# Paged latent cache and its join in a two-layer decoder step: the turned halves first, all score products in a row, the samples' output projection in four column groups

## The chip, the cores and the metric

The kernel runs on one core of one Trainium2 chip. The metric is device time in microseconds from start to end of one execution; before the change the median of three executions is 3317.36 us (3316.31 to 3318.78).

## What is computed

One inference step of a small decoder: a gated DeltaNet layer with a ConvFFN, one shared latent key/value (MLA), then an MLA attention layer with a second ConvFFN. A prompt of 1024 tokens and 16 meta tokens, and eight samples of one token each, pass through together. All inputs are float32. The part of the change is the samples' attention over their paged past, 4096 positions each in 32 pages of 128, and the output projection after it:

```python
def latent_scores(q_lat, q_pe, c, k_rope):
    s = jnp.einsum('bqhr,bkr->bhqk', q_lat, c) + jnp.einsum('bqhd,bkd->bhqk', q_pe, k_rope)
    return s.astype(jnp.float32) * MLA_SCALE

def sample_attend(q_lat, q_pe, c, k_rope, c_past, k_past):
    ...
    s_past = latent_scores(q_lat, q_pe, c_past, k_past)
    ...
    prob = jax.nn.softmax(jnp.concatenate([s_past, s_new], axis=-1), axis=-1).astype(c.dtype)
    return (jnp.einsum('bhqk,bkr->bqhr', prob[..., :P], c_past)
            + jnp.einsum('bhqk,bkr->bqhr', prob[..., P:], c))

    o = jnp.einsum('blhr,rhv->blhv', o_lat, w_uv).reshape(B, L, MLA_HEADS * MLA_V)
    return o @ w_out
```

Here r is the latent rank 256, the rope part has 64 entries, there are 8 heads, and w_out is 1024 x 1024.

## The kernel before

The program is written with a scheduler that fixes each engine's order before the run; every engine then works through its own queue strictly in that order, waiting on semaphores. `merge` gives the order in which pieces of several streams are written down: each stream yields a number, and the stream with the lowest number goes on. Near the end of the attention layer two streams are merged: `cache_all` (the samples' cache) and `outp` (the main output projection of the prompt, tile name `psop`, 576 products in three groups of heads and three chunks of tokens, accumulated into `acc`).

`cache_all` runs 16 units: eight samples b, two halves gp of 2048 positions each. `cache_unit` (L1463) does this:

- POOL gathers two blocks `cg` of 1 MB of latent rows (L1468) and one block `krt` of 0.5 MB of rope rows (L1471), through the page table. `cg` has four buffers, so two units are on the chip; `krt` has two.
- TensorE transposes `krt` in two blocks of four into PSUM (`dkt`, L1476), and VectorE copies them to `krT`.
- For each half k of the latent rank, TensorE makes 16 transposes of `cg` in four blocks (`dct_`, L1487), which ScalarE (L1491) and VectorE (L1489) copy in turn to a tile `cT` of two buffers. Then it makes four products of 32 x 512 into the score tile `dscr` (L1493), one per group j of 512 positions: the stationary side is the query, 32 columns wide, and each product uses its own 32 columns of the array (`tile_position=(0, 32 * j)`). All of `dkt`, `dct_`, `dpt` and the join's small products share three PSUM buffers (`dtr`).
- After the second half four rope products with 64 rows follow (L1497).
- Softmax over the half: row maximum (VectorE L1502), exponential with sum (ScalarE L1506), four transposes of p (`dpt`, L1510), one copy, and sixteen products p by latent (`pv`, 32 x 256, L1516), again in four column groups. `OS`, `MX` and `LS` keep the running output, maximum and sum per sample.

After the last unit `join` (L1540) runs as one piece: maxima and sums are turned (`dj`), scores of the new token are added (`dsn`), a chain of small VectorE and ScalarE steps gives the weights, which are turned (`dfw`, L1574); the groups are combined (`dol`, L1584 and L1586), the value projection follows (`dov`, L1591), and then the output projection: for each head a block `wos` of w_out (0.5 MB, two buffers, those of `krt`) is loaded by SP (L1597), and two products of 8 x 512 per head gather the eight samples' rows (`dop`, L1599). The result is copied (`ys`, L1602), turned in eight transposes (`dopt`, L1605) and stored in the first eight columns of `acc[0]`.

Behind it come the rest of `outp`, the post-norm of the three chunks (`boundaries`) and the second ConvFFN. `fpst` (L945) are transposes of state rows that this ConvFFN needs.

Of the kernel before, what the change touches and what calls it, by code (L numbers as in the profile page):

```python
# [11 lines left out]
F32 = mybir.dt.float32  # L12
# [8 lines left out]
P = 128  # L21
# [40 lines left out]
def tile_step(ctx: ExitStack, tc: tile.TileContext, I, O, stop=None):  # L62
# [1382 lines left out]
    with ExitStack() as e2:  # L1445
# [17 lines left out]
        def cache_unit(b, gp):  # L1463
# [14 lines left out]
            sc = scp.tile([P, 512], F32, tag="sc", name="dscr")  # L1478
            for k in range(2):
                yield  # L1480
                cT = sp.tile([P, 4, 512], F32, tag="cT", name="cT")
                for gg in range(2):
                    for hf in range(2):
                        pt = dtr("dct_")
                        for i in range(4):
                            o = (2 * i + hf) * KVL + P * k
                            PE.transpose(pt[:, P * i:P * i + P], cg[gg][:, o:o + P], ident)  # L1487
                        if hf:
                            V.tensor_copy(cT[:, 2 * gg + hf, :], pt)  # L1489
                        else:  # L1490
                            A.copy(cT[:, 2 * gg + hf, :], pt)  # L1491
                for j in range(4):
                    PE.matmul(sc[32 * j:32 * j + 32, :], ql[:, k, b, :], cT[:, j, :], start=(k == 0), stop=False,  # L1493
                              tile_position=(0, 32 * j))
            for j in range(4):
                hf = j % 2
                PE.matmul(sc[32 * j:32 * j + 32, :], qr_s[64 * hf:64 * hf + 64, b, :],  # L1497
                          krT[64 * hf:64 * hf + 64, j // 2, :], start=False, stop=True, tile_position=(64 * hf, 32 * j))
# [34 lines left out]
        def cache_all(p0, p1):  # L1533
            for u in range(2 * NS):
                for f, _ in enumerate(cache_unit(u // 2, u % 2)):
                    yield p0 + (p1 - p0) * (u + f / 4.0) / (2 * NS)
            yield p1
            join()

        def join():  # L1540
# [31 lines left out]
            V.tensor_tensor(sn, sn, mm, op=ALU.mult)  # L1572
            ps = dtr("dfw")
# [6 lines left out]
            V.tensor_tensor(pn, sn[:, 0:H].unsqueeze(1).to_broadcast([NS, NS, H]), bc(ident[:NS, :NS], [NS, NS, H]), op=ALU.mult)  # L1580
            olT = dc.tile([P, 2, NS, H], F32, name="olT")
            for k in range(2):
# [4 lines left out]
                V.tensor_copy(olT[:, k], ps)  # L1587
            ps = dtr("dov")[:, :H * NS].rearrange("p (h s) -> p h s", s=NS)
# [3 lines left out]
            V.tensor_copy(os_, ps)  # L1592

            ps = [dtr(f"dop{i}") for i in range(2)]
            for h in range(H):
                st = krp.tile([P, D], F32, tag="krt", name="wos")
                SP.dma_start(st, I["b_w_out"][0, P * h:P * h + P, :])  # L1597
                for i in range(2):
                    PE.matmul(ps[i][:NS, :], os_[:, h, :], st[:, 512 * i:512 * i + 512], start=(h == 0), stop=(h == H - 1))  # L1599
            yt = dc.tile([NS, D], F32, name="ys")  # L1600
            for i in range(2):
                V.tensor_copy(yt[:, 512 * i:512 * i + 512], ps[i][:NS])  # L1602
            ps = dtr("dopt")[:, :KT * NS].rearrange("p (m s) -> p m s", s=NS)
            for m in range(KT):
                PE.transpose(ps[:, m, :], yt[:, P * m:P * m + P], ident[:NS, :NS])  # L1605
            V.tensor_copy(acc[0][:, :, 0:NS], ps)
# [3 lines left out]
        os_ = dc.tile([P, H, NS], F32, name="os")  # L1610
# [5 lines left out]
        merge(cache_all(0, CA), outp(I["b_w_out"][0], og_d, groups, ogp, 0.05, 1.0, True, NS, 6))  # L1616
# [71 lines left out]
```

## Time and profile before

| | |
|---|---|
| median of three executions | 3317.36 us |
| the profiled execution | 3314.68 us, span 3312.9 us |
| TensorE busy | 3123.5 us, 94% of the span, 20846 products |
| VectorE / ScalarE / POOL busy | 2030.3 / 1254.9 / 862.2 us |
| chain that ended last | PE 76%, DVE 14%, DMA 3% |
| mean granted clock of TensorE | 0.975 of full speed |
| cache units | from 2150 us; last p-by-latent product until 2391.64 us |
| join's output projection until its result is stored | until 2440.7 us |

How to read it: the times in the rows are microseconds from the span's start, or ns where so marked. An engine is busy while one of its instructions is under way; a product that waits in the array still counts. PEld is the loading of weights into the array, which overlaps with products. A float32 product shows as two records. PEclk is the share of TensorE's full clock that was granted: 1.00 is 2.4 GHz, 0.50 is 1.2 GHz, values between them are a mix over time. SPq rows are issues of DMAs by SyncE.

### The profile page before, as it was taken

To read this page: it belongs to the slowest core of one execution; us is meant where nothing else is said; L and a number is where in the kernel's file an instruction comes from. 1 tells how busy PE (TensorE), PEld (TensorE's weight loads), DVE (VectorE), ACT (ScalarE), POOL (GpSimd) and SP (SyncE) were. 2 spreads that over 40 slices of the span, in tenths; PEclk is the share of its full clock that TensorE was granted. 3 is DMA by queue.
4 is the path that set the end of the run, shared out by engine and by line. 5 is a ranking of instruction groups with operands and counts; after the bars stand their busy time and mean duration, and the time that the engine had idled before them with its cause. 6 is when DMAs were issued, how large, how long until landed. Compare 5 with 4: busy or idle time off the path is not lost.

```text
span 3312.9 us, 52527 instructions
## 1 busy us (share of the span) xinstructions
PE 3123.5 (94%) x20846; PEld 2884.2 (87%) x20846; DVE 2030.3 (61%) x4139; ACT 1254.9 (38%) x2541; POOL 862.2 (26%) x1013
## 2 busy tenths in 40 slices
PE   7999999999899999999978999999998999999997
PEld 6888888888799999999967888856678999999996
DVE  4777777766864555555576676544557355555556
ACT  4656555563433222222334444433224322222223
POOL 1433222210342222322342111111105332322322
PEclk9999999999899999999989999999998999999999
DMA  3222222235321111111121000354432111111111
GB/s 107 62 65 69 64 67 59 72 105 176 96 66 46 39 52 49 48 46 39 45 86 44 25 27 28 108 189 184 159 102 84 46 46 45 46 45 52 46 39 66
DMA packets 267650, 235.08 MB, mean 71 GB/s; under 512 B 57919, under 2 KB 246597, under 8 KB 263285
## 3 DMA queue, kind: packets, MB, share of 16 engines
q1 hardware_dynamic: 260224, 189.69, 19.7%
q0 software_dynamic: 6912, 41.95, 3.4%
q8 instruction: 164, 2.69, 0.3%
q14 instruction: 82, 0.66, 0.1%
q10 hardware_dynamic: 268, 0.09, 0.0%
HBM read 198.84 MB, written 33.40 MB: 70 GB/s over the span
## 4 chain that ended last, share of the span: by engine, by line
PE 76%; DVE 14%; DMA 3%; issue 3%; ACT 2%; POOL 1%; SPq 0%; ACTq 0%; POOLq 0%; DVEq 0%
PE fps L228 9%; PE fps L229 9%; PE fps L227 9%; PE fdn L228 5%; PE fdn L227 5%; PE fdn L229 5%; PE psu L227 2%; PE psu L229 2%; PE po L1408 2%; PE psu L228 2%; PE dscr L1493 2%; DVE acc L287 2%; PE psop L227 1%; DVE tm L658 1%; DVE xs L660 1%
## 5 line engine op out<-in xcount | busy, mean ns | idle before, releaser
L144 POOL TENSOR_TENSOR ws<-ws,vec 128x1024 f32<-128x1024 f32 (+1 forms) x127 | 249.5, 1965 | 424.3 <-DMA ws<-in_f_w_up_dram 210.1
L228 PE MATMUL fps<-xfl,wh 128*128 128x384 f32 (+1 forms) x1056 | 343.7, 326 | 8.2 <-POOL xfl L295 8.1
L227 PE MATMUL fps<-xfh,wh 128*128 128x384 f32 (+1 forms) x1056 | 341.8, 324 | 8.0 <-ACT xfh L293 7.0
L228 PE MATMUL fps<-xbl,wh 128*128 128x384 f32 (+1 forms) x1056 | 343.6, 325 | 4.8 <-POOL xbl L295 4.7
L227 PE MATMUL fps<-xbh,wh 128*128 128x384 f32 (+1 forms) x1056 | 341.6, 324 | 1.1 <-ACT xbh L293 0.5
L229 PE MATMUL fps<-xfh,wl 128*128 128x384 f32 (+1 forms) x1056 | 342.4, 324 | 0.0
L229 PE MATMUL fps<-xbh,wl 128*128 128x384 f32 (+1 forms) x1056 | 341.2, 323 | 0.0
L966 DVE TENSOR_TENSOR fu<-fps,RS 128x384 f32<-128x384 f32 x176 | 98.0, 557 | 386.6 <-PE fps L229 386.1
L151 ACT CAST wh<-ws 128x1024 fp32r<-128x1024 f32 (+1 forms) x144 | 148.0, 1027 | 491.6 <-PE fps L228 373.8
L227 PE MATMUL fdn<-gh,dh 128*128 128x384 f32 (+1 forms) x960 | 315.2, 328 | 0.0
L228 PE MATMUL fdn<-gl,dh 128*128 128x384 f32 (+1 forms) x960 | 311.6, 325 | 0.0
L229 PE MATMUL fdn<-gh,dl 128*128 128x384 f32 (+1 forms) x960 | 308.6, 321 | 0.0
L1044 DVE TENSOR_TENSOR acc<-acc,fdn 128x384 f32<-128x384 f32 (+1 forms) x432 | 216.7, 514 | 108.8 <-PE fdn L229 108.0
L227 PE MATMUL psu<-xah,wh 128*128 128x384 f32 (+1 forms) x768 | 261.8, 341 | 9.5 <-ACT u L533 5.1
L228 PE MATMUL psu<-xal,wh 128*128 128x384 f32 (+1 forms) x768 | 260.0, 339 | 0.7 <-DVE xal L223 0.7
L229 PE MATMUL psu<-xah,wl 128*128 128x384 f32 (+1 forms) x768 | 259.0, 337 | 0.7 <-DVE wl L152 0.7
L975 DVE SCALAR_TENSOR_TENSOR fy<-fu,fcv,fy 128x1064 f32<-128x1064 f32 x176 | 238.6, 1357 | 7.6 <-ACT fy L973 7.3
L152 DVE TENSOR_TENSOR wl<-ws,wh 128x1024 fp32r<-128x1024 f32 (+1 forms) x144 | 173.6, 1206 | 71.3 <-ACT wh L151 71.1
L228 PEld LDWEIGHTS fps<-xfl,wh 128*128 128x128 f32 x1056 | 200.7, 190 | 10.8 <-POOL xfl L295 10.5
L227 PEld LDWEIGHTS fps<-xfh,wh 128*128 128x128 f32 x1056 | 200.3, 190 | 9.4 <-ACT xfh L293 7.9
L228 PEld LDWEIGHTS fps<-xbl,wh 128*128 128x128 f32 x1056 | 200.5, 190 | 6.9 <-POOL xbl L295 6.5
L227 PEld LDWEIGHTS fps<-xbh,wh 128*128 128x128 f32 x1056 | 200.2, 190 | 1.7 <-ACT xbh L293 0.9
(963 smaller groups left out, 7856.1 us busy)
## 6 DMA issues: line engine op xcount, KB each, us to landing
ws<-in_f_w_up_dram SPq DMA_DIRECT2D x88, 512.0 KB
ds<-in_f_w_down_dram SPq DMA_DIRECT2D x44, 512.0 KB
ws<-in_a_w_in_dram SPq DMA_DIRECT2D x32, 512.0 KB
xt<-in_x_prompt_dram SPq DMA_DIRECT2D x16, 512.0 KB
of<-og_d SPq DMA_DIRECT2D x32, 192.0 KB
xr<-x_d SPq DMA_DIRECT2D x16, 384.0 KB
GC<-gcd SPq DMA_DIRECT2D x24, 174.0 KB
Ss<-in_state_delta_S_dram SPq DMA_DIRECT2D x8, 512.0 KB
```

Source lines behind the costliest of these rows:

```text
L144: G.tensor_tensor(st, st, bc(fo, [P, kt, m]), op=ALU.mult)
L151: A.copy(hi, st)
L152: V.tensor_tensor(lo, st, hi, op=ALU.subtract)
L227: PE.matmul(ps, wh, ah, start=start, stop=False)
L228: PE.matmul(ps, wh, al, start=False, stop=False)
L229: PE.matmul(ps, wl, ah, start=False, stop=stop)
L287: V.scalar_tensor_tensor(a_[:, k + j, :], a_[:, k + j, :], vc(wname, k + j), res[j], op0=ALU.mult, op1=ALU.add)
L966: V.tensor_tensor(u[:, 18 + t0:18 + t0 + n], ps[:, :n], RS[:, t0:t0 + n], op=ALU.mult)
L975: V.scalar_tensor_tensor(y, u[:, j:j + LW], fcv[:, l, j, tl:tl + 1], y, op0=ALU.mult, op1=ALU.add)
L1044: V.tensor_tensor(acc[c][:, m, :], acc[c][:, m, :], ps[:, :n], op=ALU.add)
L1408: PE.matmul(po[:, :nq], vt[:kk, kb, P * (h % 2):P * (h % 2) + P], pT[:kk, j, :nq], start=(kb == 0), stop=(kb == i))
L1493: PE.matmul(sc[32 * j:32 * j + 32, :], ql[:, k, b, :], cT[:, j, :], start=(k == 0), stop=False, tile_position=(0, 32 * j))
```

## The change

Both halves of `cT` are turned and copied first; both stay until the products have read them. After a new yield all twelve score products follow in a row, in the order first latent half, rope, second latent half. `join` is a stream of its own, with yields between its steps, from the cache's end CA = 0.4 to 0.6 of the merge. The samples' output projection takes 32 columns of `os_` (24 of them cleared by POOL) as weights and puts four pieces of 256 output columns into four column groups of one PSUM tile of the `pv` pool. Its result has 128 partitions; two full transposes turn it, each copied to `acc[0]`.

```diff
@@ cache_unit @@
-            sc = scp.tile([P, 512], F32, tag="sc", name="dscr")
+            cT = []
             for k in range(2):
                 yield
-                cT = sp.tile([P, 4, 512], F32, tag="cT", name="cT")
+                t = sp.tile([P, 4, 512], F32, tag="cT", name="cT")
+                cT.append(t)
                 for gg in range(2):
                     for hf in range(2):
                         pt = dtr("dct_")
...
-                            V.tensor_copy(cT[:, 2 * gg + hf, :], pt)
+                            V.tensor_copy(t[:, 2 * gg + hf, :], pt)
                         else:
-                            A.copy(cT[:, 2 * gg + hf, :], pt)
+                            A.copy(t[:, 2 * gg + hf, :], pt)
+            yield
+
+            sc = scp.tile([P, 512], F32, tag="sc", name="dscr")
+            for k in (0, 2, 1):
                 for j in range(4):
-                    PE.matmul(sc[32 * j:32 * j + 32, :], ql[:, k, b, :], cT[:, j, :], start=(k == 0), stop=False,
-                              tile_position=(0, 32 * j))
-            for j in range(4):
-                hf = j % 2
-                PE.matmul(sc[32 * j:32 * j + 32, :], qr_s[64 * hf:64 * hf + 64, b, :],
-                          krT[64 * hf:64 * hf + 64, j // 2, :], start=False, stop=True, tile_position=(64 * hf, 32 * j))
+                    o = sc[32 * j:32 * j + 32, :]
+                    if k < 2:
+                        PE.matmul(o, ql[:, k, b, :], cT[k][:, j, :], start=(k == 0), stop=(k == 1), tile_position=(0, 32 * j))
+                    else:
+                        hf = 64 * (j % 2)
+                        PE.matmul(o, qr_s[hf:hf + 64, b, :], krT[hf:hf + 64, j // 2, :], start=False, stop=False,
+                                  tile_position=(hf, 32 * j))
             yield
@@ cache_all, join @@
-                    yield p0 + (p1 - p0) * (u + f / 4.0) / (2 * NS)
-            yield p1
-            join()
-
-        def join():
+                    yield p0 + (p1 - p0) * (u + f / 5.0) / (2 * NS)
+
+        def join(p0, p1):
+            at_ = lambda f: p0 + (p1 - p0) * f
+            yield at_(0.0)
...
+            yield at_(0.2)
             ps = dtr("dfw")
...
+            yield at_(0.3)
             olT = dc.tile([P, 2, NS, H], F32, name="olT")
...
+            yield at_(0.4)
             ps = dtr("dov")[:, :H * NS].rearrange("p (h s) -> p h s", s=NS)
...
-            V.tensor_copy(os_, ps)
-
-            ps = [dtr(f"dop{i}") for i in range(2)]
+            G.memset(os_, 0.0)
+            V.tensor_copy(os_[:, :, 0:NS], ps)
+
+            ps = pvp.tile([P, KVL], F32, tag="pv", name="dop")
             for h in range(H):
+                yield at_(0.5 + 0.05 * h)
                 st = krp.tile([P, D], F32, tag="krt", name="wos")
                 SP.dma_start(st, I["b_w_out"][0, P * h:P * h + P, :])
-                for i in range(2):
-                    PE.matmul(ps[i][:NS, :], os_[:, h, :], st[:, 512 * i:512 * i + 512], start=(h == 0), stop=(h == H - 1))
-            yt = dc.tile([NS, D], F32, name="ys")
+                for j in range(4):
+                    PE.matmul(ps[32 * j:32 * j + 32, :], os_[:, h, :], st[:, KVL * j:KVL * j + KVL], start=(h == 0), stop=(h == H - 1),
+                              tile_position=(0, 32 * j))
+            yt = dc.tile([P, KVL], F32, name="ys")
+            V.tensor_copy(yt, ps)
+            yield at_(1.0)
+            ps = dtr("dopt")
             for i in range(2):
-                V.tensor_copy(yt[:, 512 * i:512 * i + 512], ps[i][:NS])
-            ps = dtr("dopt")[:, :KT * NS].rearrange("p (m s) -> p m s", s=NS)
-            for m in range(KT):
-                PE.transpose(ps[:, m, :], yt[:, P * m:P * m + P], ident[:NS, :NS])
-            V.tensor_copy(acc[0][:, :, 0:NS], ps)
+                PE.transpose(ps[:, P * i:P * i + P], yt[:, P * i:P * i + P], ident)
+                V.tensor_copy(acc[0][:, i:KT:2, 0:NS], ps[:, P * i:P * i + P].rearrange("p (j s) -> p j s", s=32)[:, :, 0:NS])
...
-        os_ = dc.tile([P, H, NS], F32, name="os")
+        os_ = dc.tile([P, H, 32], F32, name="os")
...
-        merge(cache_all(0, CA), outp(I["b_w_out"][0], og_d, groups, ogp, 0.05, 1.0, True, NS, 6))
+        merge(cache_all(0, CA), join(CA, CA + 0.2), outp(I["b_w_out"][0], og_d, groups, ogp, 0.05, 1.0, True, NS, 6))
```

What the scheduler makes of it on TensorE, in the fifth unit of the cache (`dkt` and `dct_` transposes, `dscr` scores, `psop` main projection). Before:

```order
L228 MATMUL psop<-ogl,wh 128x384
L1487 MATMUL dct__22849<-ident,cg 128x128 x4
L1487 MATMUL dct__22855<-ident,cg 128x128 x4
L1493 MATMUL dscr<-cT,ql 32x512 x4
L1487 MATMUL dct__22866<-ident,cg 128x128 x4
L1487 MATMUL dct__22872<-ident,cg 128x128 x4
L1487 MATMUL dct__22878<-ident,cg 128x128 x4
L1487 MATMUL dct__22884<-ident,cg 128x128 x4
L1493 MATMUL dscr<-cT,ql 32x512 x4
L1497 MATMUL dscr<-krT,qr_s 32x512 x4
L229 MATMUL psop<-ogh,wl 128x384
```

The same unit in the changed kernel:

```order
L229 MATMUL psop<-ogh,wl 128x384
L1488 MATMUL dct__22848<-ident,cg 128x128 x4
L1488 MATMUL dct__22854<-ident,cg 128x128 x4
L1488 MATMUL dct__22861<-ident,cg 128x128 x4
L1488 MATMUL dct__22867<-ident,cg 128x128 x4
L1488 MATMUL dct__22873<-ident,cg 128x128 x4
L1488 MATMUL dct__22879<-ident,cg 128x128 x4
L1500 MATMUL dscr<-cT,ql 32x512 x4
L1503 MATMUL dscr<-krT,qr_s 32x512 x4
L1500 MATMUL dscr<-cT,ql 32x512 x4
L227 MATMUL psop<-ogh,wh 128x384
```

Two more blocks of transposes and the rope transposes stand ahead of either piece. The four products that stood between the two halves' transposes have moved behind all of them, and the rope products stand between the two latent sets. From eleven to seventeen projection products follow in either kernel before the softmax's transposes.

On SP, the loads of the samples' output weights (`wos`) among those of the main projection (`ws` its weights, `of` its data), from the third `wos` on. Before:

```order
L1597 DMA wos<-in_b_w_out_dram 128x1024 x2
L157 DMA ws<-in_b_w_out_dram 128x1024
L322 DMA of<-og_d_341 128x384
L1597 DMA wos<-in_b_w_out_dram 128x1024 x2
L322 DMA of<-og_d_338 128x272
L157 DMA ws<-in_f_w_up_dram 128x8x128
L1597 DMA wos<-in_b_w_out_dram 128x1024 x2
```

In the changed kernel:

```order
L1608 DMA wos<-in_b_w_out_dram 128x1024 x2
L157 DMA ws<-in_b_w_out_dram 128x1024
L1608 DMA wos<-in_b_w_out_dram 128x1024 x2
L322 DMA of<-og_d_341 128x384
L322 DMA of<-og_d_338 128x272
L1608 DMA wos<-in_b_w_out_dram 128x1024 x2
```

The load of og_d_341 stood ahead of the middle pair of `wos`; now it stands behind it. On TensorE the eight heads of `dop` stood in four pairs with 11, 12 and 10 projection products between them; now they stand one by one with 6, 15, 6, 7, 2, 13 and 6 between them. Ahead of `dfw` stood 38 projection products and two blocks of `fpst` behind the last p-by-latent product; now 33 and none, and all `fpst` blocks stand behind the main projection.

## Rows read from the trace of the kernel before

**Rows 1.** Busy us by stage: length, PE, PEld, DVE, ACT, POOL; then PEclk, DMA share, GB/s.

```profile
2172.26:2391.64 219.38, 219.13 (x1707) 132.34 (x1703) 99.61 (x215) 67.18 (x141) 38.74 (x41) 1.00 0.50 185
2402.30:2413.10 10.80, 10.80 (x58) 10.71 (x57) 0.45 (x2) 0.00 (x0) 0.00 (x0) 0.58 0.00 0
2413.10:2440.70 27.60, 25.55 (x84) 10.14 (x83) 8.48 (x14) 4.81 (x6) 2.12 (x3) 0.92 0.59 185
2440.70:2530.00 89.30, 78.71 (x432) 72.28 (x431) 70.86 (x95) 37.45 (x55) 29.60 (x17) 0.91 0.30 91
```

**Rows 2.** Timeline of TensorE over one unit: start us, us, engine, line, form, xcount.

```profile
2216.40 0.60 PE L1487 MATMUL dct__22837<-ident,cg 128*128 128x128 f32 x4
2216.84 0.60 PE L1487 MATMUL dct__22843<-ident,cg 128*128 128x128 f32 x4
2217.19 0.42 PE L228 MATMUL psop<-ogl,wh 128*128 128x384 f32 x1
...
2218.45 1.90 PE L1493 MATMUL dscr<-cT,ql 128*32 128x512 f32 x8
...
2221.67 0.66 PE L1487 MATMUL dct__22884<-ident,cg 128*128 128x128 f32 x4
2222.25 1.90 PE L1493 MATMUL dscr<-cT,ql 128*32 128x512 f32 x8
2224.08 1.06 PE L1497 MATMUL dscr<-krT,qr_s 64*32 64x512 f32 x8
2225.08 0.44 PE L229 MATMUL psop<-ogh,wl 128*128 128x384 f32 x1
2225.36 0.33 PE L227 MATMUL psop<-ogh,wh 128*128 128x384 f32 x1
2225.53 0.33 PE L228 MATMUL psop<-ogl,wh 128*128 128x384 f32 x1
...
2228.37 1.93 PE L1516 MATMUL pv<-cg,dpT 128*32 128x256 f32 x32
2230.23 0.44 PE L1476 MATMUL dkt<-ident,krt 128*128 128x128 f32 x2
```

**Rows 3.** Timeline of the weight loads (PEld), same unit; in brackets idle time and releaser.

```profile
2219.30 0.14 PEld L1493 LDWEIGHTS dscr<-cT,ql 128*32 128x32 f32 x2 [0.41 <-DVE cT L1489]
...
2223.11 0.14 PEld L1493 LDWEIGHTS dscr<-cT,ql 128*32 128x32 f32 x2 [0.48 <-DVE cT L1489]
```

**Rows 4.** Busy time by stage, the score tile dscr alone, fifteen units: us, PE, PEld, DVE, ACT.

```profile
2172.26:2391.64 219.38, 76.23 (x360) 14.88 (x360) 10.37 (x15) 11.69 (x30) 1.00 0.50 185
```

**Rows 5.** Waits of the weight loads over the fifteen units: us in total, times, longest.

```profile
PEld dscr L1493 <- DVE cT L1489: 10.3, 22, 0.5
...
PEld dscr L1493 <- ACT cT L1491: 2.9, 16, 0.4
```

**Rows 6.** Busy time, fifteen units: first the cT copies of VectorE, then of ScalarE.

```profile
2172.26:2391.64 219.38, 41.44 (x60) 1.00 0.50 185
2172.26:2391.64 219.38, 35.06 (x60) 1.00 0.50 185
```

**Rows 7.** Timeline of POOL: second gather of a unit.

```profile
2231.81 0.94 POOL L1468 DMA_INDIRECT cg<-in_cache_kv_latent_dram,idx  x1 [0.30 <-PE dct__22971 L1487]
```

**Rows 8.** The line of the latent gathers, L1468: from issue to landing.

```profile
DMA to landing us min/median/max: 5.6/7.1/9.2
```

**Rows 9.** Groups by line, join's output projection: busy us, mean ns, idle before, releasers.

```profile
L1599 PE MATMUL dop<-wos,os 128*8 128x512 f32 x32 | 16.4, 652 | 2.1 <-DMA wos<-in_b_w_out_dram 2.0
```

**Rows 10.** Timeline of SP's issues, join.

```profile
2430.54 2.04 SPq L1597 DMA_DIRECT2D wos<-in_b_w_out_dram  x2
```

**Rows 11.** Timeline of TensorE, join's output projection.

```profile
2434.79 1.88 PE L1599 MATMUL dop<-wos,os 128*8 128x512 f32 x4 [0.41 <-DMA wos<-in_b_w_out_dram]
```

**Rows 12.** Timeline of TensorE, join before the turned weights.

```profile
2397.56 0.67 PE L945 MATMUL fpst<-ident,fsrow 16*128 16x16 f32 x8
...
2399.23 0.22 PE L1574 MATMUL dfw<-ident,fw 8*128 8x8 f32 x1
```

## The prediction

> **What bounds the kernel now.** I read the table of stages first. In the stretch of the paged cache TensorE is busy 219.13 of 219.38 us at full clock, DMA is busy half the time, VectorE and ScalarE less than half [rows 1]. So TensorE's queue is the path here, and what counts is how long each step holds that queue, waits included: pieces that run on parts of the array overlap, and a late one still counts as busy. Behind the cache come two stretches in which TensorE is not quite full: the join's output projection (25.55 of 27.60 us) and the tail up to the second ConvFFN (78.71 of 89.30 us) [rows 1].
>
> The timeline of one cache unit comes next [rows 2]. The first set of four latent score products stands at 2218.45 (eight records, two per product), the second at 2222.25, the rope set at 2224.08, the next projection product at 2225.08. The four products of a set go to four column groups and could run side by side; yet the second set holds the queue for 1.83 us and the rope set for 1.00. The weight loads say why [rows 3]: the last column group's load comes only at 2219.30 and 2223.11, behind VectorE's copy of its turned block. From 2223.11 only 0.97 us remain. The rope set, whose operands have long been there, takes 1.00 us in all. So a set is about 0.98 us when its operands are ready, and the rest is waiting for copies. Over fifteen units the score tile holds TensorE for 76.23 us [rows 4], 5.08 us per unit. The waits that are put down to copies alone are 10.3 and 2.9 us [rows 5].
>
> **The change, part by part.** All against the profiled execution, span 3312.9 us and time 3314.68 us, which is 2.68 us under the median of 3317.36.
>
> *Scores in a row.* The order now has 32 transposes in eight blocks and then twelve products. When the first latent set comes, its last copy has had four more blocks of time. The second set's last copy has the first set and the rope set, 1.97 us, to finish in; a copy takes 41.44/60 = 0.69 us on VectorE and 35.06/60 = 0.58 us on ScalarE [rows 6]. Three sets then cost about 3.0 us by the way rows 4 count. Saved: 15 x (5.08 - 3.0) = 31.2 us. The first unit is released by its gathers, so I count 1.5 us there. Bounds: the p-by-latent product runs sixteen pieces of 256 columns from 2228.37 to 2230.23 without a gap, 1.86 us [rows 2]; twelve of 512 at that pace are 2.79 us and save 34.4 us. If nothing but the named waits goes, 13.2 us. I take 31.2, since the rope set is the nearest row: the same shape of product with operands ready.
>
> What sits between? The rope set starts at 2224.08, when the last latent product has finished, though the second set's first products had begun at 2222.25 [rows 2]: it was not run into the set before it. The Trainium skill, "TensorEngine Tiling (Array Packing)", Key Properties, says that changing the tiling mode drains the array; the trace agrees, with these 0.97 us, and the rule speaks against putting the 64-row set between two 128-row sets. By the rule three sets cost 2.95 us, by the pace of the p-by-latent product 2.79, over fifteen units a difference of 2.4 us.
>
> *One turn of mode less.* A block of four transposes takes 0.44 us before a like one (2216.40 to 2216.84) and 0.58 us as the last before products (2221.67 to 2222.25) [rows 2]. One such turn per unit goes: 16 x 0.14 = 2.2 us.
>
> *What hides the copies.* Eight blocks now follow each other through the same three PSUM buffers. TensorE makes two in 0.88 us; VectorE needs 0.69 and ScalarE 0.58 for one each [rows 2, 6]. That is a cover of 0.19 us per pair, and I cost it at nothing; what it costs if the cover is gone is the second rival. Both cT buffers are now full until the products have read them; the next unit writes them only after its predecessor's softmax, so this costs nothing.
>
> *Gathers.* They start when the p-by-latent product of two units earlier ends; the second of a pair is issued at 2231.81 after an end at 2230.23 [rows 2, 7]. Landing takes at most 9.2 us [rows 8], so all is there 10.8 us after that end. A unit lasts 219.38/15 = 14.6 us now and would last about 12.4: 1.6 us are left at worst. POOL's new clearing of os stands in its queue before the later gathers; POOL is busy 38.74 of 219.38 us [rows 1]. Both at nothing.
>
> *Output projection in four column groups.* It costs 16.4 us on TensorE and 2.1 us of waiting [rows 9]: eight columns of weights, 512 columns of data, one product after the other. Now a head is four pieces of 32 x 256 side by side. The nearest row, the p-by-latent product, does sixteen in 1.86 us, so four in 0.47, with the turn of mode 0.55 [rows 2]. Eight heads are 4.4 us: 12.0 us saved. But wos keeps its two buffers. A pair of loads issued from 2430.54 is awaited until 2434.79 for the first [rows 10, 11], 4.3 us. A load is issued when the head two before has read its buffer, so heads 2 to 7 need three rounds of 4.3 + 0.4 + 0.55 = 5.3 us, 16 us in all. Between them stand, by the order, 55 projection products of 0.17 us (2225.36 to 2225.53) [rows 2], 9.4 us, and 3.9 us of heads: some 3 to 4 us of waiting against 2.1. Minus 2.0 us.
>
> *Join in steps.* Today 38 projection products and two blocks of fpst, 0.67 us each, stand before dfw at 2399.23 and cover VectorE's chain of small steps [rows 12]. That chain is unchanged. Now 33 products stand there, and the fpst blocks have moved behind the projection to the others. So 5 x 0.17 + 2 x 0.67 = 2.2 us of cover are lost and run later. The small rest (two copies of ys become one, eight small transposes two full ones) lies behind five products: nothing.
>
> *Sum.* 31.2 + 1.5 + 2.2 + 12.0 - 2.0 - 2.2 = 42.7, so 3314.68 - 42.7 = 3272.0 us for such an execution and, with 2.68, **3275 us** for the median. The projection products that shorter units leave over are only moved; TensorE is the path there too. The tail keeps its order of VectorE work and shifts as a whole.
>
> **The rivals.**
>
> *The copies take over.* Eight blocks in a row stall on PSUM. For it: VectorE also has the running output and the last krT copy at the start of the run. Against it: the cover above, and the first blocks of a unit run today at 0.44 us in spite of these [rows 2]. Price: up to 1 us per unit, 16 us: 3291 us. It decides when VectorE falls more than one block behind. The Trainium skill, "TensorEngine Tiling (Array Packing)", PSUM Bottleneck, warns that after a gain on TensorE the PSUM copies may become the bound. By that rule the time is this rival's; rows 6 show the copies still under the pace.
>
> *The join gives its gain back.* The weights of the main projection's last head can be split only when older ones are released, and the long output projection has covered that chain. If this and wos are simply waited out, the join gains nothing: 3275 + 7.8 = 3283 us.
>
> *Slower: the clock.* Busy is no guarantee of clock: from 2402.30 to 2413.10 TensorE is busy throughout with products of eight columns, at a granted 0.58 [rows 1]. If the row of transposes and narrow products has the same effect, each us of it at 1.2 GHz costs 1 us more. A unit spends about 5.7 us there (six blocks and three sets); at half clock in all units that is 91 us: 3366 us. The sign turns when 43 of these 91 us are paid. Against it: today's unit has no projection product from 2217.61 to 2225.08, 7.5 us, longer than the new one, and the stretch shows 1.00 throughout [rows 1, 2].
>
> That the change does not do what it says is excluded for the scores: the order has the twelve products in a row in fifteen of sixteen units.
>
> **How the numbers follow.** Forecast 0.75, copies 0.12, join 0.08, clock 0.05. The forecast's own range: the rich end has 2.79 us per unit (3.2 us more), no waiting for wos (4 us) and a half-clock stretch shortened by some 5 us: 3263. The poor end is half way to the bound of the named waits, 9 us: 3284. With the rivals of join and copies, 3262 to 3291 us holds the time 8 times in 10. About 0.2%, 6.6 us, is what a measurement of this kernel can tell from no change. Faster then means 3310.7 or less; the first three cases are far under it, the clock case mostly over it: faster 0.93, same 0.03, slower 0.04.
>
> **What would show it.** Right: units that last 12 to 12.7 us from one p-by-latent end to the next; the score tile about 3.0 us per unit, with no wait of its weight loads for cT copies; dop under 5 us of TensorE; PEclk 1.00 through the cache. Wrong: transposes that wait for cT copies, units above 13.5 us, gathers named as what TensorE waits for, a granted clock under 1 before the join, or a tail longer than the 89.3 us that it is now.

## The result, and the profile after

The changed kernel takes **3278.07 us** (median of four, 3275.05 to 3286.42); four executions of the kernel before beside them give 3318.07 us (3316.31 to 3323.50). The ratio of the two times is 0.9881, its 95% interval 0.9859 to 0.9902; every ratio below is against executions of the kernel before made beside that run. The forecast was 3275 us with a range of 3262 to 3291. The profiled execution took 3279.13 us, span 3277.4 us. (Of one kernel below, best, the profiled execution ran at a mean granted clock of 0.80, so only its times are used.)

First the stages of the changed kernel, in the columns of [rows 1]: length, PE, PEld, DVE, ACT, POOL, PEclk, DMA share, GB/s. The lines are the fifteen units, the join's narrow products, its output projection, and a stretch of 89.30 us behind it, as long as the last line of [rows 1].

```profile
2168.75:2355.91 187.16, 186.93 (x1697) 122.62 (x1694) 97.71 (x212) 67.27 (x142) 37.46 (x40) 1.00 0.60 219
2365.40:2379.00 13.60, 13.60 (x63) 13.46 (x63) 1.11 (x4) 0.00 (x0) 0.00 (x0) 0.50 0.04 12
2379.00:2405.36 26.36, 22.61 (x142) 15.35 (x141) 7.79 (x14) 2.92 (x4) 0.74 (x1) 0.82 0.58 182
2405.36:2494.66 89.30, 76.90 (x426) 69.04 (x425) 72.07 (x96) 39.34 (x59) 30.82 (x20) 0.90 0.32 95
```

The fifteen units are 32.2 us shorter than in [rows 1] (219.38 to 187.16, 12.5 us a unit), TensorE is still full there and the clock still 1.00. The output projection's stretch is hardly shorter, and TensorE is less full in it and at a lower clock.

Now a unit's products on TensorE, to be held against [rows 2].

```profile
2196.14 0.60 PE L1488 MATMUL dct__22727<-ident,cg 128*128 128x128 f32 x4
2196.60 0.66 PE L1488 MATMUL dct__22733<-ident,cg 128*128 128x128 f32 x4
2197.09 0.60 PE L1488 MATMUL dct__22739<-ident,cg 128*128 128x128 f32 x4
2197.62 1.07 PE L1500 MATMUL dscr<-cT,ql 128*32 128x512 f32 x8
2198.61 1.06 PE L1503 MATMUL dscr<-krT,qr_s 64*32 64x512 f32 x8
2199.61 1.06 PE L1500 MATMUL dscr<-cT,ql 128*32 128x512 f32 x8
2200.60 0.45 PE L227 MATMUL psop<-ogh,wh 128*128 128x384 f32 x1
```

Each set holds the queue for 0.99 to 1.00 us; the latent sets had held it up to 1.83. The score tile alone, as in [rows 4], falls from 76.23 to 45.80 us, that is from 5.08 to 3.05 us a unit:

```profile
2168.75:2355.91 187.16, 45.80 (x360) 7.04 (x360) 10.37 (x15) 11.73 (x30) 1.00 0.60 219
```

Of the waits of the weight loads in [rows 5], those of dscr on copies of cT are gone. What stands ahead of dscr's loads now is put down to no releaser ("issue"); the copies that feed dscr appear nowhere (from 2172 to 2350 us, rows as in [rows 5]; two loads of dct wait for a copy of cT in the fifteen units, 0.2 us each):

```profile
PEld dscr L1500 <- issue: 15.1, 30, 0.8
PEld dscr L1503 <- issue: 12.6, 15, 0.8
```

In the join the output projection is the group of [rows 9], now 6.4 instead of 16.4 us, with 0.4 us of waiting for wos instead of 2.1; and TensorE's waits there have a new first line.

```profile
L1610 PE MATMUL dop<-wos,os 128*32 128x256 f32 x64 | 6.4, 480 | 0.4 <-DMA wos<-in_b_w_out_dram 0.4
```

```profile
PE psop L227 <- ACT wx L151: 3.4, 1, 3.4
PE st_ps L265 <- DVE s L259: 1.1, 1, 1.1
PE psop L227 <- DVE acc L336: 1.0, 2, 0.7
```

To apportion the time I cut every profile at four points of its own timeline: the cache's first transpose, the end of the first unit's p-by-latent product, the end of the last unit's, and the end of the main projection (the last psop). The last piece reaches to the end.

| kernel | first unit | fifteen units | join and projection | rest | sum |
|---|---|---|---|---|---|
| before | 22.08 | 219.38 | 95.63 | 825.57 | 1162.66 |
| before, second profile | 23.63 | 219.47 | 95.61 | 826.00 | 1164.71 |
| changed | 24.48 | 187.16 | 93.65 | 827.73 | 1133.02 |
| changed, second profile | 23.10 | 187.41 | 93.43 | 827.66 | 1131.60 |
| cache_only | 21.70 | 187.78 | 99.07 | 823.94 | 1132.49 |
| ready | 21.48 | 189.65 | 101.04 | 823.69 | 1135.86 |
| join_only | 23.60 | 219.68 | 87.45 | 828.85 | 1159.58 |
| groups_one_piece | 23.33 | 187.18 | 90.09 | 827.30 | 1127.90 |
| before_ws | 21.99 | 218.46 | 94.75 | 825.84 | 1161.04 |
| one_mode | 19.68 | 184.13 | 93.01 | 828.45 | 1125.27 |
| latent_first | 23.98 | 187.46 | 88.45 | 826.53 | 1126.42 |
| ws_two | 22.66 | 187.28 | 83.70 | 826.58 | 1120.22 |
| spread | 22.19 | 185.43 | 85.03 | 830.18 | 1122.83 |

From the cache on, the change is worth 29.6 us between the first two profiles and 33.1 between the second two, while the medians differ by 40.0 us in this comparison and by 36.3 in a second one below. The cache's first transpose itself comes at 2150.25 us in the profile before and at 2144.34 in the one after, in a program that is the same up to there. Over the thirteen profiles of the table that point lies between 2140.26 and 2157.18, at 2151.1 on average in the four with the old cache and at 2149.5 in the nine others. So some 30 to 33 us are shown to be the change's; the other 3 to 10 us of the medians' difference were seen in no stage that the change touches, and where they come from stays open.

The rest is longer in each of the eight profiles with the new output projection (826.53 to 830.18 us) than in any of the five with the old one (823.69 to 826.00). The two blocks of fpst that moved there, 0.67 us each [rows 12], explain a part; what the other part is stays open.

A second count helps with the units. A tile's busy time, as in [rows 4], also holds the end of its last product, under which the next tile's first has already begun. Counted from the start of each TensorE product to the start of the next, the pieces add up to the stretch. In the fifteen units the score products hold the queue in this way for 73.6 us before and 44.8 after, the transposes dct_ for 57.4 and 55.4, the projection for 36.6 and 35.3, and the p-by-latent products for 28.3 in both.

### The profile page after: what moved, and what is told of

Its sections match the earlier page's. It is cut to its first block, busy times and chain, and to the rows that moved or that the text cites. A ratio compares the mean times of both kernels' runs of the same rounds, so it can differ in the third digit from the quotient of the medians.

```text
span 3277.4 us, 52585 instructions
## 1 busy us (share of the span) xinstructions
PE 3084.6 (94%) x20872; PEld 2875.8 (88%) x20872; DVE 2032.3 (62%) x4139; ACT 1254.9 (38%) x2541; POOL 863.9 (26%) x1014
```

## The experiments

**The kernel before, once more**, for a second profile.

> The kernel before once more, with a profile, for the stretch from the cache's first transpose to the end: 1162 to 1164 us as in its first profile (2150.25 to 3312.9). If the start of the cache stands elsewhere than 2150 us, then the stages ahead of it wander from run to run by that much, in a program that is the same there.

Measured: 3319.32 us, span 3317.6. The stretch from the cache's first transpose to the end is 1164.71 us, against 1162.66, a little above the 1162 to 1164 expected, and begins at 2152.85. The stages that the change touches repeat within 0.1 us (219.47 and 95.61 against 219.38 and 95.63); what wanders lies ahead of them, and in the first unit.

**Which part brings the gain.** Three kernels with a part each, and the changed kernel again on the same chip. cache_only has the new cache unit with the old join (one piece, two products of 512 columns per head); join_only has the reverse.

> Only the cache part of the change: both latent halves turned first, twelve products in a row; the join stays one piece with two-bank output products. If the gain sits where the prediction put it, this kernel takes 31 to 35 us off the kernel before (its median 3318, so about 3285; ratio 0.989 to 0.991), the score tile holds TensorE about 3.0 us per unit, and the join's dop still costs 16 to 18 us. Rival: the cache part only moves projection products past the join and its gain is partly handed to the join; then this kernel gains 20 us or less and needs the new join for the rest.

Measured: 3289.59 us against 3317.98, ratio 0.9914 (0.9887 to 0.9940). From the cache on it gains 30.2 us: 31.6 in the fifteen units, while join and projection are 3.4 us longer, 2.0 of it twelve more projection products of 0.17 us (355 against 343). The first theory holds at its lower edge (28.4 us by the medians, where 31 to 35 were expected); the rival, by which the gain is handed on to the join, does not.

> Only the join part of the change: join in steps, output projection in four column groups; the cache unit is that of before, dscr about 5.1 us per unit. Prediction's terms for this part: 12.0 gained, 2.0 and 2.2 lost, so 7 to 8 us off the kernel before (about 3310; ratio 0.9975). What the trace of the whole change suggests is less: 31 more projection products between the last unit and dopt, 5.3 us, of which the new wait on the last head's weights is already taken. Rival (the join gives its gain back): no more than 2 us either way.

Measured: 3309.21 us, ratio 0.9972 (0.9952 to 0.9991). Join and projection fall from 95.63 to 87.45 us, 8.2 us, with 343 projection products in either; behind that 2.9 to 3.3 us are given back, by the two profiles of before. So the join alone is worth about 5 us, less than the 7.8 of the sum, which had counted what runs later; the medians, with 3 to 16 us by their interval, cannot tell. Beside the new cache the join's stretch gains only 2.0 us (95.63 to 93.65).

> The changed kernel once more, on the same chip as the three runs beside it, to compare them with: 3275 to 3281 us, ratio about 0.988.

Measured: 3281.71 us (3274.87 to 3286.91), ratio 0.9883 (0.9848 to 0.9918). Its join again has the long wait, 3.6 us.

**Waiting for copies, or the long row?** ready keeps the old number of turns between transposes and products and moves only their places:

```diff
 blocks(0, 0); blocks(0, 1)
-latent(0)
 blocks(1, 0)
+latent(0)
 blocks(1, 1)
-latent(1)
 rope()
+latent(1)
```

(blocks(k, g) are two blocks of transposes with their copies, latent(k) four products; these names stand for the loops of the cache unit.)

> The join is that of before and the cache keeps its five changes between transposes and products per unit; only the place of the products moves: the first latent set stands after the first half of the second set of transposes, and the rope set ahead of the second latent set, so that no product stands right behind the copies it reads. Theory (what the row of products saves is waiting for copies): the score tile falls from 5.1 to about 3.1 us per unit, and the kernel gains 25 to 31 us (about 3290; ratio 0.991). Rival (the long row itself, with fewer changes of mode, is what saves): the score tile stays at 4.5 us or more per unit and the gain is under 10 us.

Measured: 3283.96 us, ratio 0.9894 (0.9860 to 0.9927); from the cache on it gains 26.8 us. The score tile of its fifteen units, in the columns of [rows 4], and the waits on copies that are left:

```profile
2175.45:2365.11 189.66, 48.40 (x360) 7.33 (x360) 10.38 (x15) 11.71 (x30) 1.00 0.59 216
```

```profile
PEld dscr L1494 <- issue: 14.1, 28, 0.8
...
PEld dscr L1494 <- DVE cT L1488: 1.2, 1, 1.2
```

27.8 of the 30.4 us that the score tile lost are won without a single product more in the row. It was waiting for the copies. Of the other 2.6 us (48.40 against 45.80; over the stretch 189.66 against 187.16) 1.9 lie in the second unit alone, with the wait of 1.2 us for one copy: it lasts 14.17 us, and 12.26 in the changed kernel. In the fourteen units behind it the score products, from start to start, hold the queue for 41.8 us in either, where it was 68.5 before. What the fifth turn of mode costs there is in the transposes, 52.2 against 51.7 us.

**What a change of tile shape costs.** one_mode makes the rope products over all 128 rows; half of the queries' rows are zeros, so the sums are the same.

```diff
+qz = dc.tile([P, 2, NS, 32], F32, name="qz")
+G.memset(qz, 0.0)
+for d_ in range(2):
+    V.tensor_copy(qz[64 * d_:64 * d_ + 64, d_], qr_s[64 * d_:64 * d_ + 64])
...
-hf = 64 * (j % 2)
-PE.matmul(o, qr_s[hf:hf + 64, b, :], krT[hf:hf + 64, j // 2, :], ..., tile_position=(hf, 32 * j))
+PE.matmul(o, qz[:, j % 2, b, :], krT[:, j // 2, :], ..., tile_position=(0, 32 * j))
```

> The changed kernel with the rope keys' four products made over all 128 rows (the queries' other 64 rows are zeros), so that the twelve products of a unit have one shape of tile. Theory (a set of another shape waits for the set before it and is waited for): the three sets fall from 2.98 to about 2.75 us, 3.7 us over sixteen units, about 3275 where the changed kernel has 3279. Rival (four products of 512 columns take 0.97 us whatever stands ahead of them): no change within 1 us in the stretch of the cache.

Measured: 3270.60 us, ratio 0.9867 (0.9844 to 0.9890). A unit's three sets, and the score tile of the fifteen:

```profile
2177.12 1.06 PE L1505 MATMUL dscr<-cT,ql 128*32 128x512 f32 x8
2178.00 1.04 PE L1507 MATMUL dscr<-krT,qz 128*32 128x512 f32 x8
2178.86 1.04 PE L1505 MATMUL dscr<-cT,ql 128*32 128x512 f32 x8
```

```profile
2159.94:2344.07 184.13, 42.63 (x360) 10.28 (x360) 10.37 (x15) 11.72 (x30) 1.00 0.62 223
```

The second set now starts 0.88 us after the first and the third 0.86 after that, where it was 0.99 and 1.00. The tile loses 3.2 us and the stretch 3.0, with one projection product more in it (196 against 195). The trace agrees with the rule that the prediction drew from the Trainium skill, "TensorEngine Tiling (Array Packing)", Key Properties; here it is some 0.11 to 0.14 us per change of shape. By the full time alone this could not be told, since the intervals of the two kernels overlap.

latent_first changes only the order of the sets, `for k in (0, 2, 1)` to `for k in range(3)`.

> The changed kernel with the order first latent set, second latent set, rope set. Theory: the shape of tile changes once less between sets, so a unit gains about 0.1 us if the second latent set's copies are done when it comes, 1 to 2 us in all; if the rope set between them is needed as cover, the second set waits for its last copy 0.3 to 0.5 us per unit and the kernel loses 5 to 8 us.

Measured: 3279.09 us, ratio 0.9874 (0.9848 to 0.9900). The two latent sets run as one piece of 1.85 us, as the first theory has it, but the second set's weight loads wait for copies after all:

```profile
2205.18 1.92 PE L1500 MATMUL dscr<-cT,ql 128*32 128x512 f32 x16
2207.03 1.06 PE L1503 MATMUL dscr<-krT,qr_s 64*32 64x512 f32 x8
```

```profile
PEld dscr L1500 <- DVE cT L1490: 3.5, 13, 0.3
PEld dscr L1500 <- ACT cT L1492: 2.1, 1, 2.1
```

The first of these two lines is thirteen waits of at most 0.3 us, one per unit; the products are not held up by them. The single 2.1 us stands in the second unit. There ScalarE's copy is queued behind a split of the main projection's weights, and that split behind a load:

```profile
2179.79 1.04 ACT L151 CAST wx<-ws 128x1024 fp32r<-128x1024 f32 x1 [2.14 <-DMA ws<-in_b_w_out_dram]
2180.74 0.58 ACT L1492 COPY cT<-dct__22441 128x512 f32<-128x512 f32 x1
```

That unit lasts 14.07 us instead of the changed kernel's 12.26, so the stretch is no shorter (187.46 against 187.16, with three more projection products in it). In the fourteen units behind it the score products hold the queue, from start to start, for 39.9 us against 41.8: 0.14 us a unit, the price of the one change of shape that is saved. In one_mode, which saves two, it is 38.0. So the first theory holds where the copies come in time, and the one late copy takes the gain back. The join of latent_first is 5.2 us shorter than the changed kernel's, with six projection products fewer and a wait of 1.2 us for wx where that has 3.4. The next runs show what stands behind that.

**The new wait in the join.** In the changed kernel the chain behind the 3.4 us can be followed through three engines: TensorE, then ScalarE, then SP's issues.

```profile
2388.89 0.45 PE L227 MATMUL psop<-ogh,wx 128*128 128x384 f32 x1
2389.17 0.34 PE L228 MATMUL psop<-ogl,wx 128*128 128x384 f32 x1
2389.35 0.34 PE L229 MATMUL psop<-ogh,wx 128*128 128x384 f32 x1
2393.08 0.69 PE L227 MATMUL psop<-ogh,wx 128*128 128x384 f32 x1 [3.39 <-ACT wx L151]
2393.57 0.52 PE L228 MATMUL psop<-ogl,wx 128*128 128x384 f32 x1
2393.89 0.52 PE L227 MATMUL psop<-ogh,wx 128*128 128x384 f32 x1
```

```profile
2384.08 1.05 ACT L151 CAST wx<-ws 128x1024 fp32r<-128x1024 f32 x1 [23.51 <-PE psop L228]
...
2391.98 1.04 ACT L151 CAST wx<-ws 128x1024 fp32r<-128x1024 f32 x1 [6.02 <-DMA ws<-in_b_w_out_dram]
```

```profile
2386.42 0.33 SPq L157 DMA_DIRECT2D ws<-in_b_w_out_dram  x1
```

The weights of the last two heads can be split only when TensorE has released older ones, at 2384.08. The two share one staging buffer, ws: the second load is issued at 2386.42, when VectorE has read the first, and the split starts when it has landed, at 2391.98. Behind the wait the same projection products start 0.32 us apart instead of 0.17. ws_two gives every second head of this projection a staging buffer of its own:

```diff
+if out is None or not skip or i % 2 == 0:
     ws.append(wprep(wg, src, KT, P, out=out))
+else:
+    st = pool.tile([P, KT * P], F32, tag="ws2", name="ws2", bufs=1).rearrange("p (k m) -> p k m", k=KT)
+    SP.dma_start(st, src)
+    ws.append(wsplit(wg, st, KT, P, None, "w", out))
```

> The changed kernel with a second staging buffer for the output projection's weights, so that the last head's weights can be loaded while the head before is split. Theory (TensorE's 3.4 to 3.6 us wait for ScalarE's wx between the heads of the output projection is the new bound of the join): that wait goes, the stretch from the last p-by-latent product to dopt falls from 49 to 45 or 46 us, and the whole by 3 us, to about 3276. Rival: the wait moves to the loads of wos or behind the join, and the time stays.

Measured: 3269.63 us, ratio 0.9854 (0.9834 to 0.9874). The second split now follows the first, and of TensorE's waits in join and projection this is all that is left:

```profile
2393.62 1.05 ACT L151 CAST wx<-ws 128x1024 fp32r<-128x1024 f32 x1 [21.92 <-PE psop L228]
...
2394.99 1.05 ACT L151 CAST wx<-ws 128x1024 fp32r<-128x1024 f32 x1
```

```profile
PE dop L1619 <- DMA wos<-in_b_w_out_dram: 0.7, 3, 0.3
```

The gain is larger than the wait: join and projection fall from 93.65 to 83.70 us, with 355 projection products in either. The table of stages, from the last p-by-latent product to dopt, shows why. The first line is before, the second the changed kernel, the third ws_two.

```profile
2391.71:2440.71 49.00, 46.95 (x217) 30.16 (x217) 16.65 (x41) 6.27 (x10) 2.22 (x4) 0.86 0.38 117
```

```profile
2355.98:2405.36 49.38, 45.53 (x258) 36.93 (x259) 16.50 (x42) 4.38 (x8) 0.84 (x2) 0.76 0.34 108
```

```profile
2367.12:2412.11 44.99, 44.22 (x272) 36.41 (x272) 18.19 (x44) 6.91 (x11) 2.50 (x3) 0.85 0.37 115
```

The granted clock of the stretch is 0.86, 0.76 and 0.85. Where it was lost, in the same columns: the first two lines are the changed kernel, the next two its second profile, the last two ws_two.

```profile
2364.85:2381.91 17.06, 17.06 (x82) 15.98 (x81) 1.99 (x6) 0.00 (x0) 0.00 (x0) 0.50 0.04 13
2392.15:2398.98 6.83, 5.90 (x26) 3.41 (x27) 2.24 (x3) 0.88 (x1) 0.00 (x0) 0.50 0.59 199
```

```profile
2374.92:2388.57 13.65, 13.65 (x67) 12.59 (x66) 1.76 (x5) 0.00 (x0) 0.00 (x0) 0.50 0.01 2
2398.81:2405.64 6.83, 5.83 (x26) 3.34 (x27) 2.24 (x3) 0.95 (x1) 0.00 (x0) 0.50 0.58 206
```

```profile
2377.97:2391.63 13.66, 13.66 (x67) 12.60 (x66) 1.76 (x5) 0.00 (x0) 0.00 (x0) 0.50 0.01 2
2391.63:2450.82 59.19, 58.49 (x371) 50.48 (x372) 41.85 (x68) 22.53 (x33) 5.76 (x3) 1.00 0.45 137
```

The stretch at 0.50 among the narrow products stands in every kernel, ahead of the wait. The second one begins in the last us of the wait, in both profiles of the changed kernel, and ws_two has none. TensorE is busy for 5.90 us of it, half of which is lost. So the late weights cost 3.4 us of waiting and some 3 us of clock. The other 3.6 us of the gain are a first stretch at 0.50 that was longer in this profile, though not in the second one (1.7 us), and smaller waits, mostly on VectorE, that are gone too.

Was that limit there before, hidden by the long output projection? before_ws is the kernel before with the same edit.

> The kernel before with the second staging buffer for the output projection's weights that ws_two has. Theory (in the kernel before the long output projection hides that chain, so the limit was made visible by the change): 3 us or less is gained, ratio 0.999 or more, and the stretch from the last p-by-latent product to the end of psop stays at 94 to 96 us. Rival (the chain bounds the join in both kernels): 7 to 10 us are gained as in ws_two, and that gain has nothing to do with the change.

Measured: 3309.32 us against 3313.58, ratio 0.9996 (0.9980 to 1.0011); join and projection 94.75 against 95.63 us. The chain costs next to nothing in the kernel before. The change brought it to light.

**Groups or steps.** groups_one_piece keeps the four column groups and puts the join back into one piece: the `yield at_(...)` lines go, and join() is called once, when the last unit is through.

> The changed cache and the output projection in four column groups, but the join in one piece as before. It tells the groups from the steps. If the groups alone bring what the join part is worth, the stretch from the last p-by-latent product to the end of the projection (psop) is about 94 us, as in the changed kernel, against 99 us with the old output projection (cache_only), and the time is near the changed kernel's 3279. If the steps matter (their projection products between the heads give the loads of wos their time), TensorE waits 4 us or more for wos and the time is 3282 or more.

Measured: 3276.12 us, ratio 0.9875 (0.9853 to 0.9898). Join and projection take 90.09 us, against 99.07 in cache_only (the old output projection) and 93.65 in the changed kernel. TensorE waits 0.9 us for wos and 1.7 for wx. So the groups bring 9.0 us and the steps cost 3.6. Of these 1.7 are the longer wait for wx. Here one more head stands ahead of the projection product that waits, and the load of the last head's weights, issued at 2387.96, is there for the split after 4.4 us instead of 5.6. What makes up the other 1.9 us was not followed. The groups alone do better than the first theory had it, and the steps were not needed for wos.

**Together.** best is one_mode with ws_two; spread also lets projection products in between the value products of the join and spreads its steps further (`join(CA, CA + 0.3)`, two more yields).

> one_mode and ws_two together: the changed kernel with rope products over 128 rows and the second staging buffer. They act in different stretches (the cache; the join), so from the first transpose of the cache to the end 6 to 8 us and 11 to 12 us should add up: about 1114 us there where the changed kernel has 1132, and a median of 3262 to 3265. Rival: a shorter cache makes the weights late again, and no more than ws_two's gain is left.

Measured: 3272.76 us, ratio 0.9865 (0.9841 to 0.9888). That the two gains add up isn't shown: the time is that of either alone. Whether its rival is the reason stays open.

> best, with the join spread over more of the projection: projection products also stand inside the samples' value products (dov), and the heads of the output projection stand further apart. Theory (narrow products without projection products between them bring the clock down, to 0.50 to 0.58 over 13 us): the granted clock of the join rises above 0.85 and 2 to 4 us are gained over best. Rival: the clock falls all the same, or the later end of the join delays the statistics behind it; no gain or a loss of up to 4 us.

Measured: 3263.53 us, ratio 0.9844 (0.9826 to 0.9862). It is the fastest here, 50 us under the kernel before; the changed one has a ratio of 0.9881. But not for the reason given:

```profile
2362.32:2417.30 54.98, 53.17 (x307) 45.91 (x307) 22.68 (x51) 10.45 (x17) 5.79 (x4) 0.81 0.41 122
```

The granted clock of its join is 0.81, not above 0.85, and by the table its way from the cache to the end, 1122.83 us, is no shorter than that of ws_two, 1120.22. Its rest, 830.18 us, is the longest of all, as the second half of the rival has it. Whether spread is better than ws_two or best stays open; the intervals overlap.

## Why the prediction was right, and where its sum was too rich

In the cache the mechanism was right, and so were the sign and the time: 3278.07 against 3275. That the time came so near is in part luck. The sum promised 42.7 us; from the cache on the profiles show 29.6 and 33.1, with 32.2 and 32.1 in the fifteen units, and the medians' difference of 40.0 holds some 7 to 10 us that no stage of the change shows. The join, 7.8 us in the sum, brought next to nothing: its stretch is 2.0 to 2.2 us shorter and the rest behind it 1.7 to 2.2 us longer. By its steps:

- **Scores in a row, 31.2 us.** Right in cause and nearly in size. The score tile lost 30.4 us by the count of rows 4, 3.05 us a unit against the 3.0 expected, and 28.8 from start to start. ready shows the cause: there the same is won without a longer row. Against 2.95 us by the rule and 2.79 by the pace, three sets took 2.98 from start to start; with one shape, in one_mode, 2.77.
- **One turn of mode less, 2.2 us.** From start to start the transposes lost 2.0 us in the fifteen units, where the term put it. But 1.4 of it come in ready too, which has the old number of turns; the turn itself is worth about 0.6. The fifteen units are 32.2 us shorter, of which eight projection products of 0.17 us were only moved (203 of them before, 195 now): 30.9 us against 33.4.
- **First unit, 1.5 us.** It gained nothing that two profiles each can show: 22.08 and 23.63 before, 24.48 and 23.10 after, with four projection products fewer in it. The premise was wrong: it is not the gathers that release this unit. TensorE waits for ScalarE's first copy of cT, 2.1 us before and 3.7 after, and that copy stands in ScalarE's queue behind data of the main projection that have not landed:

```profile
2149.44 0.51 ACT L324 CAST ogh<-of 128x384 fp32r<-128x384 f32 x1 [4.54 <-DMA of<-og_d]
2149.85 0.58 ACT L1492 COPY cT<-dct__22292 128x512 f32<-128x512 f32 x1
```

- **Copies and gathers at nothing.** Right for the fifteen units: the units lost nearly what the sum said, and no gather is named as what TensorE waits for. The rival of the copies did not come. What can make a copy late is not the pace of the blocks but a load that holds up the copying engine ahead of it, as in the first unit, and in the second of ready and latent_first.
- **Output projection in four groups, 12.0 us.** 10.0 by the group itself (16.4 to 6.4), 9.0 net by cache_only against groups_one_piece; the sum had 12.0. A head holds the queue for 0.57 us at full clock (2388.32 to 2388.89), near the 0.55 assumed, but for 1.01 where the clock is low (2394.66 to 2395.67).
- **Waiting for wos, 2.0 us more.** This step failed. The wait fell, from 2.0 to 0.4 us (from 1.8 to 1.0 in the second profiles). The loads ran under the projection products between the heads, in the steps and in one piece (0.9 us) alike; only in join_only was it longer, 2.7 us. The term was also above its own working, by which 16 less 9.4 less 3.9 leaves 2.7 us of waiting, 0.6 more than the 2.1 before.
- **Lost cover of the steps, 2.2 us.** The steps cost 3.6, by another way than the prediction said: half of it is the longer wait for the last head's weights. The two fpst blocks, which only moved, are paid behind the projection; the rest grew from 825.57 to 827.73 us (826.00 to 827.66 in the second profiles).
- **The join gives its gain back.** A rival with 0.08, and its first half is what happened: the weights of the last head were late. In join_only, with the long units, the join's stretch gains 8.2 us, about 5 with what runs later. Beside the shorter units the stretch's gain shrank to 2.0 us, or 4.0 with the twelve projection products of 0.17 us that it also took over (355 against 343), before what the rest lost. The prediction priced the wait of wos and left this one to a rival; it did not price the clock.
- **Slower: the clock.** In the cache it stayed at 1.00, as argued. In the join it fell a second time, behind a wait.

Of the signs named ahead, units of 12.48 us, no waits of dscr on cT, 3.05 us for the score tile and a clock of 1.00 came; dop under 5 us did not (6.4).

## What to carry to other kernels

Products that read a copy should stand a few blocks behind it; where they stand is worth more than how many are in a row. A copy is late, however short, when its engine is held up by a load ahead of it. When a long stretch on the critical engine is made short, list the chains that it has hidden, here a single staging buffer, and price each as a term of the sum: the wait, and the clock that is lost after it. And cut two profiles of each kernel at the same points before believing a difference of medians: here the stages ahead of the change wandered by 17 us.

## What the runs showed that was not expected

The wait of 3.4 us cost more than itself. The narrow products run at 0.50 in either kernel, TensorE busy throughout (13.66 us from 2403.96 before, the 13.60 us shown above after), but behind the wait the projection products start 0.32 us apart, as they would at 1.2 GHz, until the clock is 1.00 again from 2398.98. A second stretch at 0.50 stands behind waits of 1.7 to 3.6 us in both profiles of the changed kernel and in groups_one_piece, one_mode and join_only. Not every wait is followed by one: before_ws waits 1.8 us for wos without it. In ws_two, without that wait, the last 12 us ahead of dopt were granted in full:

```profile
2400.00:2412.10 12.10, 11.71 (x83) 8.80 (x82) 3.89 (x7) 2.64 (x3) 2.39 (x2) 1.00 0.74 234
```

In the changed kernel the 12 us between the wait and dopt were granted 0.76:

```profile
2393.08:2405.36 12.28, 12.28 (x70) 8.33 (x71) 3.85 (x7) 0.00 (x0) 0.74 (x1) 0.76 0.59 183
```

And products over rows that are half zeros were cheaper than products over half the rows, since the first need no change of tile shape.
